# A float32 decoder layer on one core: some hidden tiles are split into halves ahead of DRAM, and the planner's numbers are set anew

## The chip, the cores and the metric

The kernel runs on one core of one Trainium2 chip. The metric is the device time of one execution in microseconds (us); lower is better. The engines are named PE (TensorE, the matmuls), PEld (its weight loads), DVE (VectorE), ACT (ScalarE), POOL (GpSimd) and SP (SyncE, which here issues most of the DMAs). DVE, ACT, POOL, SP and PE each run their own queue of instructions in order, and wait for each other by semaphores.

## The reference

One inference step of one decoder layer, for a prompt of 1024 tokens and 8 sample tokens that share the weights (1032 token columns, `T`; half of them with the samples is `TW` = 520, `HALF` is 512). `D_MODEL` is 1024, `D_FF` is 2816 (22 tiles of 128).

```python
def layer(x, pool_hist, conv_hist, start_pos, mk, mv, ...):
    h = rmsnorm(x, g_mix)
    u = h @ w_in
    a, val, gate = ...                       # 512 columns each
    glu = val * jax.nn.sigmoid(gate)
    ya = pool_mixer(a_ext, ...)              # window means 2/4/8/16, then a linear map for each group
    yb = conv_mixer(g_ext, ...)              # depthwise conv of width 31, LayerNorm, silu
    x = x + jnp.concatenate([ya, yb], axis=-1) @ w_out
    x = x + cross_attn(rmsnorm(x, g_attn), mk, mv, w_q, w_o)      # 4 heads, 256 memory tokens
    h = rmsnorm(x, g_ffn)
    x = x + (jax.nn.silu(h @ w_gate) * (h @ w_up)) @ w_down
    return x, ...
```

The memory's K and V are `rmsnorm(mem) @ w_k` and `@ w_v` for the prompt, and come from a cache for the samples. A last RMSNorm gives the outputs; all is float32.

## The kernel before, in words

**Precision.** Each matmul runs as three passes, high by high, high by low and low by high (`PASSES`). So each operand is held as two halves, in an operand tile (`op_r`, tag `op`, of which there are 19). Function `split` makes them: a copy to the high half (L400, on ACT or POOL) and a subtract to the low half (L411, on DVE or POOL). Function `split_by_dma` spares DVE: ACT writes the high half and its negative (L422), and a DMA on POOL's queue adds the source once more from DRAM onto the negative (L429), which leaves the low half.

**Order.** Nothing is issued in the order of the source. Each operation is recorded with its cost on each engine that could do it, and a planner lists them by priority, with the text `ORDER` as the order of the pieces, and with leads (`LEAD`), factors on the costs (`MARGINS`), `SLACK` and `BIAS` that say how far ahead a load or a split is put. The outcome is one fixed list for each engine; buffers of a tag (`op` 19, `raw` 3, `scr` 3, `acc` 1) go round among tiles as they come free.

**Stages.** First the projections and mixers (pieces A, m, g, v, s, C, D, M, W), with the memory's K (K0 to K3: matmuls `kps<-memg,w` L891, evacuated to `kf` by DVE L895) and V beside them, up to about 200 us of the span. There DVE also does the depthwise convolution: taps (L725), for the samples a short set (`side`, `cs`, `y`, L681 to L684), window sums (`win`, L855 to L869). Then output projection, attention (`pv`, evacuated to `oo` by L1131) up to about 537 us.

**Gated tiles** (pieces S, T, P and the rest up to about 931 us): 22 tiles of the hidden dimension, each by seven products over halves of the tokens and of the model (a Strassen-type scheme; functions `seven` and `others`). `to_hidden` stores the result: of the first 16 tiles, in pairs, seven blocks for each chunk of four tiles to DRAM `hb` (`to_blocks`; block numbers A11 = 4, S1 = 3, A12 = 0, S2 = 5, S3 = 6, S4 = 2, A22 = 1), of the last six (16 to 21) plain values to DRAM `hd`.

**Down stage** (o, u, x, y pieces, about 920 to 1070 us): 16 units, `down(u)`, chunk `u // 4`, four units for each. A unit loads a raw block of w_down (`dr`, tag `raw`), makes four sums and differences (`dt`, L1555, on POOL or DVE), and splits `dt` into `dV` and `dr` into `dW`. `down_blocks` loads the seven blocks of a chunk (`hs<-hb`, a scratch tile) and splits each into an operand tile `hb`. Which of them go through `split_by_dma` is in this line of it:

```python
            if b in DOWN_ORDER[: (0, 2, 4, 4)[c]]:
```

The products (`pr`, L1371) are evacuated into `x` and `pp` by DVE (L1387, added) or ACT (L1391, copied). **Last stage:** `hidden_load` loads the last six tiles (`ht<-hd`) and splits them by DMA into `ho`; `last_down` multiplies them (`fd` L1714), and the final norm writes `out_yT`.

Of the kernel before, what the change touches and what calls it, by code (L numbers as in the profile page):

```python
# [74 lines left out]
TW = HW[1]  # L75
A12, A22, S4, S1, A11, S2, S3 = range(7)
# [185 lines left out]
def hybrid_step_kernel(ctx: ExitStack, tc: tile.TileContext, io):  # L262
# [29 lines left out]
    def f32(ap):  # L292
        return ap.bitcast(F32)
# [81 lines left out]
    def dma(out, in_, nbytes, r=(), w=()):  # L375

        add({"SP": 0.05}, lambda e: e.dma_start(out(), in_()), r, w, nbytes=nbytes)
# [39 lines left out]
    def split_by_dma(dst, key, src, n, r, again, again_keys, pool_too=False):  # L417


        def scaled(e, p, src, factor):  # L420
            if e is nc.scalar:
                e.activation(dst(p), src, AF.Copy, scale=factor)  # L422
            else:
                e.tensor_scalar(dst(p), src, factor, 1.0, ALU.mult, ALU.mult)

        either = {"ACT": act(n), "Pool": pool_ts(n)} if pool_too else {"ACT": act(n)}
        add(either, lambda e: scaled(e, 0, src(), 1.0), r, [key(0)])
        add(either, lambda e: scaled(e, 1, f32(dst(0)), -1.0), [key(0)], [key(1)])
# [1001 lines left out]
    def kept(f, q):  # L1430

        return lambda: he[f][:, q]

    def times_value(f, q):
        if f in he:
            combine(kept(f, q), (he[f], q), part(f, q), (su[f], q), part(f, 2 + q), (su[f], 2 + q), ALU.mult, HW[q])
        else:
            times(f, q, part(f, 2 + q), (su[f], 2 + q))

    def to_blocks(f, first, count, src, keys):  # L1440
        c, j = f // 4, f % 4 // 2
# [136 lines left out]

# [51 lines left out]
    hops = []  # L1630

    def hidden_load(f):
        t = scr(f"ht{f}", (P, 2, TW))
        dma(lambda: t[:], lambda: hd[f - FIRST_LAST], 8 * P * TW, r=[("hd", f)], w=[(t,)])
        ho = op_r(f"ho{f}", (P, 2, 2, TW))
        split_by_dma(lambda p: ho[:, p], lambda p: (ho, p), lambda: t[:], 2 * TW, [(t,)], lambda: hd[f - FIRST_LAST], [("hd", f)])
        hops.append(ho)
# [258 lines left out]
```

## Time and profile before

| | us |
|---|---|
| median of three runs | 1162.25 |
| the runs | 1160.59, 1162.25, 1166.04 |
| the profiled execution | 1161.49 |
| its span | 1159.6 |
| PE busy | 1125.3 (97%) |
| DVE busy | 926.2 (80%) |
| ACT busy | 522.6 (45%) |
| POOL busy | 247.6 (21%) |
| mean granted clock of PE | 0.997 |

Busy is the time in which an engine has an instruction in work, over the whole span. A row of the timeline reads: start, length, engine, line, operation, output and inputs, shape, count; a bracket at its end says how long the engine stood idle just before it and what ended that. A row of the table by stage gives busy us and instruction count for each engine in a stretch.

### The profile page before, as it was taken

What the parts mean: (1) busy time and instruction counts of PE and PEld (TensorE: products, weight loads), DVE (VectorE), ACT (ScalarE), POOL (GpSimd) and SP (SyncE); (2) the same over time, 40 slices, a digit from 0 to 9 for tenths busy, and PEclk for the clock granted to TensorE, in tenths of its full rate; (3) what the DMA queues carried; (4) which work ended last, traced back from release to release, by engine and by line L of the source; (5) the groups of instructions that cost most, each with busy time, mean ns of one, the idle gap of its engine ahead of it and who ended that gap; (6) DMA issues with size and microseconds to landing.
All of it is one profiled execution on the core that took longest, in us unless ns stands there. A gap on an engine that the chain in (4) does not pass through costs nothing.

```text
span 1159.6 us, 19434 instructions
## 1 busy us (share of the span) xinstructions
PE 1125.3 (97%) x7736; PEld 1067.6 (92%) x7736; DVE 926.2 (80%) x1548; ACT 522.6 (45%) x718; POOL 247.6 (21%) x297
## 2 busy tenths in 40 slices
PE   9999989999999989999999999999999999999996
PEld 8899978999999979998999999999999999888996
DVE  7999999867359886879888887788867797879744
ACT  7666647455135552554232322233222455544633
POOL 3569853131101102122000000000000124332101
PEclk9999999999999999999999999999999999999999
DMA  7235595526386776422332233322323698678712
GB/s 303 75 81 126 114 253 172 194 81 204 134 282 201 230 250 247 124 79 74 119 120 83 106 132 112 119 83 102 129 76 131 229 296 237 169 195 218 172 56 92
DMA packets 60170, 179.69 MB, mean 155 GB/s; under 512 B 7792, under 2 KB 11568, under 8 KB 58800
## 3 DMA queue, kind: packets, MB, share of 16 engines
q1 hardware_dynamic: 53392, 157.56, 38.8%
q0 software_dynamic: 6256, 20.54, 10.2%
q8 instruction: 60, 0.98, 0.4%
q10 hardware_dynamic: 432, 0.36, 0.1%
q14 instruction: 30, 0.25, 0.1%
HBM read 144.66 MB, written 33.78 MB: 154 GB/s over the span
## 4 chain that ended last, share of the span: by engine, by line
PE 58%; DVE 12%; DMA 8%; issue 4%; ACT 2%; POOL 1%; SPq 0%; DVEq 0%; POOLq 0%; ACTq 0%
PE pr L1371 38%; PE po L512 5%; PE fd L1714 4%; PE ob L512 4%; PE oa L512 3%; DMA dr<-in_w_dn 3%; PE ps L512 2%; DMA xa<-x1d 1%; DVE x L1387 1%; DVE spcache_k L1165 1%; DMA hs<-hb 1%; DVE spcache_v L1165 1%; PE vps L969 1%; DVE hb L411 1%; DVE dV L411 1%
## 5 line engine op out<-in xcount | busy, mean ns | idle before, releaser
L1371 PEld LDWEIGHTS pr<-ab,wTb 128*128 128x128 f32 x1056 | 124.4, 190 | 2.2
L1371 PE MATMUL pr<-ab,wTa 128*128 128x260 f32 x1056 | 125.2, 275 | 0.9 <-DVE su L1387 0.9
L1371 PEld LDWEIGHTS pr<-ab,wTa 128*128 128x128 f32 x1056 | 123.1, 190 | 2.3 <-DVE su L1387 1.1
L1371 PE MATMUL pr<-ab,wTb 128*128 128x260 f32 x1056 | 124.8, 275 | 0.0
L1371 PE MATMUL pr<-ab,wG 128*128 128x512 f32 x528 | 121.2, 380 | 0.4 <-DVE wG L411 0.4
L512 PE MATMUL ps<-xop,w 128*128 128x344 f32 x720 | 106.0, 310 | 2.5 <-DVE w L411 1.5
L1371 PEld LDWEIGHTS pr<-ab,wG 128*128 128x128 f32 x528 | 96.6, 189 | 12.6 <-DVE wG L411 0.8
L512 PEld LDWEIGHTS ps<-xop,w 128*128 128x128 f32 x720 | 105.0, 189 | 3.0 <-DVE w L411 1.7
L1387 DVE TENSOR_TENSOR su<-pr,su 128x520 f32<-128x520 f32 (+1 forms) x112 | 77.4, 692 | 36.6 <-PE pr L1371 35.3
L1371 PEld LDWEIGHTS pr<-hb,dV 128*128 128x128 f32 x768 | 93.1, 190 | 4.4 <-DVE x L1387 1.9
L1371 PE MATMUL pr<-hb,dV 128*128 128x260 f32 x768 | 93.7, 275 | 1.5 <-DVE x L1387 1.5
L512 PE MATMUL ps<-xq,w 128*128 128x344 f32 x576 | 88.0, 311 | 1.0 <-DMA w<-in_w_q 1.0
L512 PEld LDWEIGHTS ps<-xq,w 128*128 128x128 f32 x576 | 84.2, 189 | 1.3 <-DMA w<-in_w_q 1.3
L512 PEld LDWEIGHTS po<-oo,w 128*128 128x128 f32 x576 | 84.0, 189 | 0.9 <-DVE oo L1131 0.6
L512 PE MATMUL po<-oo,w 128*128 128x344 f32 x576 | 84.5, 310 | 0.3 <-DVE oo L1131 0.2
L725 DVE SCALAR_TENSOR_TENSOR cacc<-glu,vec,cacc 128x511 f32<-128x511 f32 (+14 forms) x116 | 76.9, 740 | 0.0
L1371 PE MATMUL pr<-hb,dW 128*128 128x512 f32 x288 | 70.7, 382 | 4.9 <-DVE x L1387 3.8
L400 ACT ACTIVATE w<-raw 128x1024 fp32r<-128x1024 f32 (+1 forms) x37 | 35.0, 949 | 74.3 <-PE po L512 21.0
L1398 POOL MEMSET su<- 128x16 f32 x22 | 2.4, 111 | 294.0 <-PE pr L1371 248.8
L1714 PE MATMUL fd<-ho,w 128*128 128x260 f32 (+1 forms) x432 | 64.3, 311 | 0.0
L1714 PEld LDWEIGHTS fd<-ho,w 128*128 128x128 f32 x432 | 59.8, 190 | 4.4 <-issue 0.5
L1371 PEld LDWEIGHTS pr<-hb,dW 128*128 128x128 f32 x288 | 50.8, 189 | 11.0 <-DVE x L1387 4.1
(311 smaller groups left out, 2173.0 us busy)
## 6 DMA issues: line engine op xcount, KB each, us to landing
gr<-in_w_gu SPq DMA_DIRECT2D x44, 512.0 KB, 3.3
hb<-su SPq DMA_DIRECT2D x8, 1040.0 KB, 4.6
hs<-hb SPq DMA_DIRECT2D x16, 520.0 KB, 5.0
dr<-in_w_dn SPq DMA_DIRECT2D x16, 512.0 KB, 5.2
spcache_k<-in_cache_k SPq DMA_DIRECT2D x12, 512.0 KB, 5.8
hs<-hb SPq DMA_DIRECT2D x12, 512.0 KB, 5.9
raw<-in_w_in SPq DMA_DIRECT2D x10, 512.0 KB, 4.1
hb<-he SPq DMA_DIRECT2D x8, 520.0 KB, 2.8
```

What stands on the lines that cost most here:

```text
L400: e.activation(dst(0), src(), AF.Copy, scale=1.0 if gain is None else gain)
L411: e.tensor_tensor(dst(1), src(), f32(dst(0)), ALU.subtract)
L512: e.matmul(placed(ps[:, c, :CW]), w[:, wi, cols], turns(x[:, xi, c * CW : (c + 1) * CW]), start=first and p == 0, stop=last and p == 2)
L725: e.scalar_tensor_tensor(acc[h][:, n:], src[:, : HALF - n], w, acc[h][:, n:], ALU.mult, ALU.add)
L969: e.matmul(placed(ps[:, m]), memg[k // 4][:, xi, k % 4, m * P : (m + 1) * P], turns(w[:, wi, col : col + 512]), start=(k == 0 and p == 0), ...
L1165: e.scalar_tensor_tensor(piece[:, b], piece[:, b], 1.0, bc[:, b], ALU.mult, ALU.mult, accum_out=out(m)[:, first + b : first + b + 1])
L1371: e.matmul(placed(bank(c)), w[:, wi, cols(j)], turns(xs[0](j, xi)[:, c * n : (c + 1) * n]), start=onto is None and j == 0 and p == 0, stop ...
L1387: from_sums(sums, "DVE", dve, lambda e, src, sl: e.tensor_tensor(as_banks(o(sl), src), src, as_banks(a(sl), src), op), [akey], [okey])
L1398: add({"Pool": 0.12}, lambda e: e.memset(o(), 0.0), [], keys)
L1714: e.matmul(placed(view(i)), w[:, wi, col : col + P], turns(hops[k][:, xi, half, lo - half * HALF + i * width // count : lo - half * HALF + ...
```

## The change

The matmuls stay the same in kind and number. Three things change.

1. Of the last six gated tiles, five (17 to 21) are split before they are stored, and of the blocks for the down stage six: 2, 3 and 6 of chunk 1, 6 of chunk 2, 4 and 5 of chunk 3. A new function `split_here` does it: ACT copies the high half to a tile of tag `acc`, DVE subtracts it in place, and both halves are stored. They are loaded as they are into the operand tile, by two DMAs of SP, with no work of ACT, DVE or POOL behind. `hd` and `hb` in DRAM get a dimension for the half.
2. Which blocks are split by DMA add: the first 0, 1, 0 and 5 of `DOWN_ORDER` for chunks 0 to 3, instead of 0, 2, 4 and 4. As blocks 4 and 5 of chunk 3 are split ahead, the adds that are really issued are 0, 1, 0 and 3. (The entries 0 and 1 that `BY_DMA` gains for `w_in` change nothing: these two blocks go through another function.)
3. The planner's numbers: `ORDER`, `LEAD`, `BIAS`, `SLACK`, `MARGINS`. PE's two cost constants only get names.

By the order of the instructions, DVE has 13 more (nine subtracts of 1040 columns, four of 520; low halves of `hb` stay 18 in all, 7, 3, 6 and 2 for the chunks instead of 7, 5, 3 and 3); adds `hb<-hb` fall from 10 to 4, `ho<-hd` from 6 to 1; SP has 26 more DMAs.

```diff
-BY_DMA = {"w_in": (3, 4, 6, 7, 9, 10, 11), "w_k": (2, 3, 5), "w_o": (4, 5, 6), "w_out_a": (1,), "w_out_b": (3,), "w_q": (4, 5, 6), "w_v": (0, 7), "w_dn": (18, 19), "w_dn2": (1,)}
+BY_DMA = {"w_in": (0, 1, 3, 4, 6, 7, 9, 10, 11), "w_k": (2, 3, 5), "w_o": (4, 5, 6), "w_out_a": (1,), "w_out_b": (3,), "w_q": (4, 5, 6), "w_v": (0, 7), "w_dn": (18, 19), "w_dn2": (1,)}
-LEAD = {"w_k": 2, "w_v": 3, "w_out_a": 15, "w_q": 15, "w_in": 1, "w_out_b": 12, "w_o": 8}
+LEAD = {"w_k": 2, "w_v": 4, "w_out_a": 14, "w_q": 26, "w_in": 6, "w_out_b": 11, "w_o": 9}
-BIAS = {"evac": 0, "prep": 40, "load": 0}
+BIAS = {"evac": 0, "prep": 60, "load": 0}
+DOWN_BY_DMA = (0, 1, 0, 5)
+SPLIT_BLOCKS = ((), (2, 3, 6), (6,), (4, 5))
+SPLIT_FIRST = (17, 18, 19, 20, 21)
-SLACK = {"Pool": 0.3, "ACT": 0.15, "DVE": 0.05, "PE": 0.05}
+SLACK = {"Pool": 0.214, "ACT": 0.15, "DVE": 0.043, "PE": 0.051}
-    "down": {"DVE": (1.0, 0.083)},
+    "down": {"DVE": (0.97, 0.083)},
...
+    def split_here(name, n, src, keys):
+        hi = buf(name, "acc", (P, n, TW), F32R)
+        add({"ACT": act(n * TW)}, lambda e: e.activation(hi[:], src(), AF.Copy), keys, [(hi,)])
+        add({"DVE": dve(n * TW)}, lambda e: e.tensor_tensor(src(), src(), f32(hi[:]), ALU.subtract), keys + [(hi,)], keys, lock=True)
+        return hi
...
     def down_blocks(c, which):
+            if b in SPLIT_BLOCKS[c]:
+                o = db[c, b] = op_r(f"hb{c}_{b}", (P, 2, 2, n))
+                for p in range(2):
+                    dma(lambda o=o, p=p: f32(o[:, p]), lambda again=again, p=p: again(p=p), 8 * P * n,
+                        r=[("hb", c, b, j, p) for j in range(2)], w=[(o, p)])
+                continue
...
-            if b in DOWN_ORDER[: (0, 2, 4, 4)[c]]:
-                split_by_dma(part, key, src, 2 * n, [(t,)], again, [("hb", c, b, j) for j in range(2)])
+            if b in DOWN_ORDER[: DOWN_BY_DMA[c]]:
+                split_by_dma(part, key, src, 2 * n, [(t,)], again, kept_keys)
...
     def hidden_load(f):
+        if f in SPLIT_FIRST:
+            for p in range(2):
+                dma(lambda p=p: f32(ho[:, p]), lambda p=p: hd[f - FIRST_LAST, p], 8 * P * TW, r=[("hd", f, p)], w=[(ho, p)])
+            return
```

How the order moves shows at three places (names carry a chunk, unit or tile number and then the number of the tile's buffer; the lines of the changed kernel are four higher).

SP's queue in the down stage, before: from the raw weight of unit 6 (`dr6`) to that of unit 7 (`dr7`), with the loads `hs2_` of chunk 2 between them.

```order
L377 DMA dr6_9576<-in_w_dn 128x1024 [waits DMAHW0_49,DMAHW4_49,DVE_49,Pool_49]
L377 DMA hs2_4_9624<-hb_85 128x2x512 [waits DMAHW7_49,DVE_49,Activation_49]
L377 DMA hs2_3_9638<-hb_85 128x1040 [waits DMAHW2_49,DVE_49]
L377 DMA hs2_0_9657<-hb_85 128x2x512 [waits DMAHW3_49,DVE_49]
L377 DMA hs2_5_9670<-hb_85 128x1040 [waits DMAHW5_49,Activation_49]
L377 DMA hs2_6_9696<-hb_85 128x1040 [waits DMAHW6_49,DMAHW1_49,Activation_49]
L377 DMA dr7_9701<-in_w_dn 128x1024 [waits DVE_49]
```

The same place in the changed kernel, where `hb1_6` and `hb1_2` are operand tiles of chunk 1 that are loaded as halves:

```order
L381 DMA dr6_9611<-in_w_dn 128x1024 [waits DMAHW0_49,DVE_49,Pool_49]
L381 DMA hb1_6_9627<-hb_85 128x1040 [waits DMAHW5_49,PE_49]
L381 DMA hb1_6_9627<-hb_85 128x1040 [waits DMAHW6_49]
L381 DMA hb1_2_9639<-hb_85 128x2x512 [waits DMAHW7_49,PE_49]
L381 DMA hb1_2_9639<-hb_85 128x2x512
L381 DMA hs2_0_9679<-hb_85 128x2x512 [waits DMAHW1_49,DVE_49]
L381 DMA dr7_9705<-in_w_dn 128x1024 [waits DMAHW2_49,DVE_49]
```

Between the two raw weights there are five loads as before, but four of them are halves for chunk 1 and wait for PE, and most of chunk 2's loads have moved elsewhere. Ahead of `dr11` five loads become six, ahead of `dr15` three become five.

ACT's queue around the first evacuation of the down stage (`x2_0<-pr`), before:

```order
L400 ACTIVATE dW1_9211<-dr1_9007 128x256
L400 ACTIVATE hb0_2_9222<-hs0_2_9124 128x1024 [waits DMAHW1_49]
L400 ACTIVATE dV1_9226<-dt1_9180 128x1024 [waits DVE_49,Pool_49]
L400 ACTIVATE hb0_1_9236<-hs0_1_9155 128x1040 [waits DMAHW2_49]
L1391 ACTIVATE x2_0_9116<-pr2556_9228 128x512 [waits DMAHW0_49,PE_49]
L1423 ACTIVATE su21_8971<-su21_8971 128x520 [waits DVE_49,Activation_49]
```

And now:

```order
L404 ACTIVATE dW1_9256<-dr1_9051 128x256
L404 ACTIVATE hb0_2_9270<-hs0_2_9200 128x1024 [waits DMAHW7_49]
L1395 ACTIVATE x2_0_9161<-pr2597_9274 128x512 [waits PE_49]
L1427 ACTIVATE su21_8885<-su21_8885 128x520 [waits DVE_49,Activation_49]
L404 ACTIVATE dV1_9329<-dt1_9224 128x1024 [waits Pool_49]
L404 ACTIVATE hb0_1_9337<-hs0_1_9261 128x1040 [waits DMAHW5_49]
```

The evacuation now comes ahead of the copies for `dV1` and `hb0_1`.

DVE's queue around the low half of the third weight tile of K2's group (`w20`), before:

```order
L725 SCALAR_TENSOR_TENSOR cacc3_1_1482<-glu2_993,vec_68,cacc3_1_1482 128x499 [waits DVE_49]
L725 SCALAR_TENSOR_TENSOR cacc3_0_1477<-glu2_993,vec_68,cacc3_0_1477 128x498 [waits DVE_49]
L725 SCALAR_TENSOR_TENSOR cacc3_1_1482<-glu2_993,vec_68,cacc3_1_1482 128x498 [waits DVE_49]
L725 SCALAR_TENSOR_TENSOR cacc3_0_1477<-glu2_993,vec_68,cacc3_0_1477 128x497 [waits DVE_49]
L855 COPY win3_1648<-win3_1648 128x2x4 [waits Pool_49]
L856 TENSOR_TENSOR win3_1648<-win3_1648 128x2x508
L411 TENSOR_TENSOR w20_1673<-raw20_1590,w20_1673 128x1024 [waits DMAHW0_49,Activation_49]
L867 TENSOR_TENSOR win3_1648<-win3_1648,cnt_75 128x2x8 [waits DVE_49]
```

And now, the rows up to it (its own, `L415 ... w20`, is the next):

```order
L415 TENSOR_TENSOR kT0_1656<-kf1_1714,kT0_1656 128x512 [waits Activation_49]
L859 COPY win3_1679<-win3_1679 128x2x2 [waits Pool_49]
L860 TENSOR_TENSOR win3_1679<-win3_1679 128x2x510
L685 COPY side_216<-glu2_992 128x8
L686 TENSOR_TENSOR cs2_1747<-side_216,vec_68 128x248 [waits DVE_49]
L687 TENSOR_REDUCE y2_1122<-cs2_1747 128x8 [waits DVE_49]
L688 TENSOR_SCALAR y2_1122<-y2_1122,vec_68 128x8 [waits DVE_49]
L859 COPY win3_1679<-win3_1679 128x2x4
L860 TENSOR_TENSOR win3_1679<-win3_1679 128x2x508
L871 TENSOR_TENSOR win3_1679<-win3_1679,cnt_75 128x2x8 [waits DVE_49]
L872 TENSOR_REDUCE win3_1679<-side_216 128x8
L873 SCALAR_TENSOR_TENSOR win3_1679<-win3_1679,a1_531 128x1032 [waits DVE_49]
```

The low half of `kT`, one sample convolution and a window's mean (L871 to L873) are now ahead of the weight's low half, and in turn they no longer stand behind it.

More of the change, by code (lines that the diff above doesn't have):

```diff
@@ L41 @@
 ORDER = (
[5 rows of a table removed]
[5 rows of a table added]
 )
-BY_DMA = {"w_in": (3, 4, 6, 7, 9, 10, 11), "w_k": (2, 3, 5), "w_o": (4, 5, 6), "w_out_a": (1,), "w_out_b": (3,), "w_q": (4, 5, 6), "w_v": (0, 7), "w_dn": (18, 19), "w_dn2": (1,)}
+BY_DMA = {"w_in": (0, 1, 3, 4, 6, 7, 9, 10, 11), "w_k": (2, 3, 5), "w_o": (4, 5, 6), "w_out_a": (1,), "w_out_b": (3,), "w_q": (4, 5, 6), "w_v": (0, 7), "w_dn": (18, 19), "w_dn2": (1,)}
 WIDE = ("w_k", "w_v")
-LEAD = {"w_k": 2, "w_v": 3, "w_out_a": 15, "w_q": 15, "w_in": 1, "w_out_b": 12, "w_o": 8}
+LEAD = {"w_k": 2, "w_v": 4, "w_out_a": 14, "w_q": 26, "w_in": 6, "w_out_b": 11, "w_o": 9}
 LAST_SPANS = ((0, 512), (512, 260), (772, 260))
-BIAS = {"evac": 0, "prep": 40, "load": 0}
+BIAS = {"evac": 0, "prep": 60, "load": 0}
 ALL_SAMPLES = (1, 6, 7)
+DOWN_BY_DMA = (0, 1, 0, 5)
+SPLIT_BLOCKS = ((), (2, 3, 6), (6,), (4, 5))
+SPLIT_FIRST = (17, 18, 19, 20, 21)
+PE_FIXED, PE_COLUMN = 0.0135, 0.000417
 SCORES_MM = (12, 13, 14, 15)
-SLACK = {"Pool": 0.3, "ACT": 0.15, "DVE": 0.05, "PE": 0.05}
+SLACK = {"Pool": 0.214, "ACT": 0.15, "DVE": 0.043, "PE": 0.051}
 MARGINS = {
     "early": {"PE": (0.93, 0.0), "DVE": (0.93, 0.0), "Pool": (1.0, 0.0), "ACT": (1.0, 0.0)},
-    "gated": {"Pool": (1.02, 0.0), "DVE": (1.0, 0.04), "PE": (0.97, 0.0), "ACT": (1.1, 0.0)},
-    "down": {"DVE": (1.0, 0.083)},
-    "last": {"PE": (0.93, 0.0), "DVE": (1.0, 0.083)},
+    "gated": {"Pool": (0.99, 0), "DVE": (1.02, 0.04), "PE": (0.98, 0), "ACT": (1.08, 0)},
+    "down": {"DVE": (0.97, 0.083)},
+    "last": {"PE": (0.94, 0.08), "DVE": (1.03, 0.123)},
 }
@@ L317, in pe @@
     def pe(n, count=1):
-        return (0.0135 + 0.000417 * n) * count
+        return (PE_FIXED + PE_COLUMN * n) * count
     def pe32(n):
@@ L352, in hybrid_step_kernel @@
     x2d = dram.tile([KT, P, T], F32, name="x2d")
-    hd = dram.tile([FF_TILES - FIRST_LAST, P, 2, TW], F32, name="hd")
-    hb = dram.tile([CHUNKS, 7, P, 2, TW], F32, name="hb")
+    hd = dram.tile([FF_TILES - FIRST_LAST, 2, P, 2, TW], F32, name="hd")
+    hb = dram.tile([CHUNKS, 2, 7, P, 2, TW], F32, name="hb")
     qd = dram.tile([HEADS, NS, 256], F32, name="qd")
@@ L1438, in times_value @@
             times(f, q, part(f, 2 + q), (su[f], 2 + q))
+    def split_here(name, n, src, keys):
[3 more added lines that the diff above has]
+        return hi
     def to_blocks(f, first, count, src, keys):
         c, j = f // 4, f % 4 // 2
-        dma(lambda: hb[c, first : first + count, :, j].rearrange("b p t -> p b t"), src, 4 * P * TW * count, r=keys,
-            w=[("hb", c, b, j) for b in range(first, first + count)])
+        parts = [(first, count)] if not any(b in SPLIT_BLOCKS[c] for b in range(first, first + count)) else [
+            (b, min(2, first + count - b)) for b in range(first, first + count, 2)]
+        for b, n in parts:
+            at, pk = (lambda b=b, n=n: src()[:, b - first : b - first + n]), keys[b - first : b - first + n]
+            if b in SPLIT_BLOCKS[c]:
+                hi = split_here(f"bh{f}_{b}", n, at, pk)
+                dma(lambda b=b, n=n: hb[c, 0, b : b + n, :, j].rearrange("b p t -> p b t"), lambda hi=hi: f32(hi[:]), 4 * P * TW * n,
+                    r=[(hi,)], w=[("hb", c, x, j, 0) for x in range(b, b + n)])
+            dma(lambda b=b, n=n: hb[c, 1, b : b + n, :, j].rearrange("b p t -> p b t"), at, 4 * P * TW * n, r=pk,
+                w=[("hb", c, x, j, 1) for x in range(b, b + n)])
     def start(f, q, single=ms_buf):
@@ L1485, in to_hidden @@
             combine(kept(e, 1), (he[e], 1), kept(e, 0), (he[e], 0), part(f, 3), (k, 3), ALU.subtract)
+            combine(part(f, 2), (k, 2), part(f, 0), (k, 0), kept(e, 1), (he[e], 1), n=HALF)
             to_blocks(f, A11, 2, lambda: he[e][:], [(he[e], 0), (he[e], 1)])
-            combine(part(f, 2), (k, 2), part(f, 0), (k, 0), kept(e, 1), (he[e], 1), n=HALF)
             to_blocks(f, A12, 4, lambda: su[f][:], [(k, q) for q in range(4)])
@@ L1492, in to_hidden @@
         else:
-            dma(lambda: hd[f - FIRST_LAST], lambda: su[f][:, 0:2], 8 * P * TW, r=[(k, 0), (k, 1)], w=[("hd", f)])
+            whole = [(k, 0), (k, 1)]
+            if f in SPLIT_FIRST:
+                hi = split_here(f"hh{f}", 2, lambda: su[f][:, 0:2], whole)
+                dma(lambda: hd[f - FIRST_LAST, 0], lambda: f32(hi[:]), 8 * P * TW, r=[(hi,)], w=[("hd", f, 0)])
+            dma(lambda: hd[f - FIRST_LAST, 1], lambda: su[f][:, 0:2], 8 * P * TW, r=whole, w=[("hd", f, 1)])
     def seven(f):
@@ L1568, in down_blocks @@
             n = WIDTH[b]
+            again, kept_keys = (lambda b=b, n=n, p=1: hb[c, p, b][:, :, :n]), [("hb", c, b, j, 1) for j in range(2)]
+            if b in SPLIT_BLOCKS[c]:
+                o = db[c, b] = op_r(f"hb{c}_{b}", (P, 2, 2, n))
[3 more added lines that the diff above has]
+                continue
             t = scr(f"hs{c}_{b}", (P, 2, n))
-            again = lambda b=b, n=n: hb[c, b][:, :, :n]
-            dma(lambda t=t: t[:], again, 8 * P * n, r=[("hb", c, b, j) for j in range(2)], w=[(t,)])
+            dma(lambda t=t: t[:], again, 8 * P * n, r=kept_keys, w=[(t,)])
             o = db[c, b] = op_r(f"hb{c}_{b}", (P, 2, 2, n))
             part, key, src = (lambda p, o=o: o[:, p]), (lambda p, o=o: (o, p)), (lambda t=t: t[:])
-            if b in DOWN_ORDER[: (0, 2, 4, 4)[c]]:
-                split_by_dma(part, key, src, 2 * n, [(t,)], again, [("hb", c, b, j) for j in range(2)])
+            if b in DOWN_ORDER[: DOWN_BY_DMA[c]]:
+                split_by_dma(part, key, src, 2 * n, [(t,)], again, kept_keys)
             else:
@@ L1632, in hidden_load @@
     def hidden_load(f):
+        ho = op_r(f"ho{f}", (P, 2, 2, TW))
+        hops.append(ho)
+        if f in SPLIT_FIRST:
+            for p in range(2):
+                dma(lambda p=p: f32(ho[:, p]), lambda p=p: hd[f - FIRST_LAST, p], 8 * P * TW, r=[("hd", f, p)], w=[(ho, p)])
+            return
         t = scr(f"ht{f}", (P, 2, TW))
[L1634 to L1637, printed above, removed]
+        dma(lambda: t[:], lambda: hd[f - FIRST_LAST, 1], 8 * P * TW, r=[("hd", f, 1)], w=[(t,)])
+        split_by_dma(lambda p: ho[:, p], lambda p: (ho, p), lambda: t[:], 2 * TW, [(t,)], lambda: hd[f - FIRST_LAST, 1], [("hd", f, 1)])
     parts = {
```

10 rows, old and new, of the table ORDER are left out of this document.

## The prediction

> **What bounds the kernel now.** I read the page first (who is busy), then the table by stage (where TensorE, PE, stands idle), then PE's own waits in those stages, and last the queue behind each wait. All durations are from the profiled execution: 1161.49 us with a span of 1159.6, which is 0.76 under the median of the three runs, 1162.25.
>
> The page's first part, and the table by stage (start and end; then busy us and instruction count of PE, its weight loads, DVE, ACT, POOL; PE's granted clock; DMA share; GB/s):
>
> ```profile
> PE 1125.3 (97%) x7736; PEld 1067.6 (92%) x7736; DVE 926.2 (80%) x1548; ACT 522.6 (45%) x718; POOL 247.6 (21%) x297
> ...
> 90.00:200.00 110.00, 104.59 (x674) 97.77 (x674) 108.09 (x163) 66.60 (x83) 72.15 (x55) 0.98 0.62 163
> 537.00:931.00 394.00, 393.86 (x2826) 373.63 (x2826) 321.20 (x449) 120.08 (x156) 7.55 (x36) 1.00 0.34 119
> 931.00:1068.00 137.00, 130.82 (x923) 122.96 (x924) 118.09 (x172) 72.66 (x91) 47.17 (x54) 1.00 0.78 216
> ```
>
> PE bounds the kernel: 34 us of the span (1159.6 - 1125.3) are not PE, and the matmuls are the same after the change. So every gain is one of PE's idle stretches. Three stages matter. 90 to 200 us: DVE is busy 108.09 of 110, so DVE's queue sets the end there and PE's waits are its echo. 537 to 931, the gated tiles: PE lacks 0.14 us in all. 931 to 1068, most of the down stage: PE lacks 6.2. PE's waits there, in brackets with what ended them:
>
> ```profile
> 931.95 1.56 PE L1371 MATMUL pr<-hb,dW 128*128 128x512 f32 x6 [1.09 <-ACT x L1391]
> 985.26 1.53 PE L1371 MATMUL pr<-hb,dW 128*128 128x512 f32 x6 [0.21 <-DVE x L1387]
> 989.74 1.56 PE L1371 MATMUL pr<-hb,dW 128*128 128x512 f32 x6 [1.60 <-DVE x L1387]
> 1024.58 1.61 PE L1371 MATMUL pr<-hb,dV 128*128 128x260 f32 x12 [1.47 <-DVE x L1387]
> 1029.13 1.56 PE L1371 MATMUL pr<-hb,dW 128*128 128x512 f32 x6 [0.32 <-DVE x L1387]
> 1058.87 1.56 PE L1371 MATMUL pr<-hb,dW 128*128 128x512 f32 x6 [1.64 <-DVE x L1387]
> ```
>
> They sum to 6.33. Five of the six name DVE's evacuation of PSUM (L1387), but DVE itself waited. Rows of the queues of POOL and DVE, then SP's, then the chain of waits (start, length, kind):
>
> ```profile
> 1021.41 0.73 POOL L1555 TENSOR_TENSOR dt<-dr 128x256 f32<-128x256 f32 x1 [8.12 <-DMA dr<-in_w_dn]
> 983.58 0.93 DVE L1555 TENSOR_TENSOR dt<-dr,dt 128x256 f32<-128x256 f32 x1 [3.06 <-POOL dt L1555]
> 1056.04 0.43 DVE L1555 TENSOR_TENSOR dt<-dr 128x256 f32<-128x256 f32 x1 [2.06 <-DMA dr<-in_w_dn]
> ...
> 963.31 7.75 SPq L377 DMA_DIRECT2D hs<-hb  x5
> 971.11 6.18 SPq L377 DMA_DIRECT2D dr<-in_w_dn  x2
> 1001.77 7.95 SPq L377 DMA_DIRECT2D hs<-hb  x5
> 1009.80 6.28 SPq L377 DMA_DIRECT2D dr<-in_w_dn  x2
> 1041.16 4.45 SPq L377 DMA_DIRECT2D ht<-hd  x3
> ...
> 971.11 10.74 DMA dr<-in_w_dn
> 1009.80 11.45 DMA dr<-in_w_dn
> 1048.87 7.05 DMA dr<-in_w_dn
> ```
>
> So one story is told three times: a chunk's loads `hs` go out in a burst, the raw weight `dr7` (then `dr11`, `dr15`) is issued behind them, lands 10.74, 11.45 and 7.05 us later, the sum `dt` waits for it in the queue of POOL or DVE, and the evacuations that PE needs stand behind that sum. The two slow landings have software adds `hb<-hb` beside them, in the third stretch only one `ho<-hd` is.
>
> **The change, part by part.**
>
> *Splits in the gated stage* (13 times a high copy on ACT and a low subtract on DVE: nine of 1040 columns, four of 520). DVE's subtract of 1040 took 1.23 and a 512-wide form 0.68 (rows below), so 9 x 1.23 + 4 x 0.68 = 13.8 us of DVE, and 9 x 1.05 + 4 x 0.57, about 12, of ACT (a copy of 1024 or 1040 columns and one of 512, below). Both have the room: in 394 us DVE is idle 72.8 and ACT 274. What hides it is PE's own work of 393.86; if DVE were late at a tile's end, each 1.23 would show. The last split (tile 21) falls after 931, where DVE is all but full; chunk 1 has two lows fewer on DVE there (3 for 5, -2.5). Cost 0; bounds 0 and +2.5 (two 1040 subtracts on a full DVE).
>
> ```profile
> 962.02 1.23 DVE L411 TENSOR_TENSOR hb<-hs,hb 128x1040 fp32r<-128x1040 f32 x1
> 970.58 0.68 DVE L1387 TENSOR_TENSOR x<-pr,x 128x512 f32<-128x512 f32 x1
> 930.37 1.05 ACT L400 ACTIVATE hb<-hs 128x1040 fp32r<-128x1040 f32 x1
> 931.33 0.57 ACT L1391 ACTIVATE x<-pr 128x512 f32<-128x512 f32 x1
> 930.00:960.00 30.00, 28.91 (x208) 27.27 (x207) 28.99 (x44) 18.14 (x26) 8.73 (x10) 1.00 0.90 275
> ```
>
> *The evacuation on ACT at 931.* PE waited 1.09 for `x`, which stood behind a `dV` copy and an `hb` copy (1.05). In the new order it comes ahead of both. -1.09; bounds -1.09 and 0 (if the next evacuation, on DVE, is as late).
>
> *Adds that go.* Adds of `hb` fall from 10 to 4 and of `ho` from 6 to 1: 11 x 0.52 = 5.7 MB leave the software queue, and as much is loaded by SP instead. From 900 to 1160 us:
>
> ```profile
> q1 hardware_dynamic: 14321, 37.48, 41.1%
> q0 software_dynamic: 3376, 10.05, 22.5%
> ```
>
> A software MB takes 22.5/10.05 = 2.24% of the engines in these 260 us, a hardware MB 1.10%; 5.7 x 1.14 = 6.5%, about 17 us of engine time, comes free. None of it is on PE's path except through `dr`:
>
> First stall (`dr7`). Still five loads lie between `dr6` and `dr7`, but no add is left in chunk 2 to share the engines; and two of DVE's lows, for which the old burst waited, are gone. A landing like the third one (7.05 for 10.74) is 3.7 us earlier, more than the 3.06 that DVE waited. -1.81; bounds -1.81 and 0.
>
> Second (`dr11`). Six loads for five lie ahead, and three of the four adds of chunk 3 stay; DVE gets 6 lows for 3 in chunk 2. Half: -0.9; bounds -1.79 and +1.5 (one more load, 7.95/5 = 1.6).
>
> Third (`dr15`). One `ht` and four `ho` lie ahead for three `ht`: 0; bounds -1.64 and +3.0 (two loads of 4.45/3).
>
> *The new wait.* `hs` went into a scratch tile freed by ACT or DVE. A direct `hb` or `ho` goes into an operand tile that PE must have released, so SP's queue stands until then, and behind it stand the next `hs` and `dr`. No row of before shows this; nearest is a `dr` stall (1.6 on PE), in up to five places. I take +0.5, as the order leaves several groups of PE between load and use; bounds 0 and +8.
>
> *The early stage.* The first 34 us are the same. Behind that, DVE's rows (start, length):
>
> ```profile
> 83.78 0.76 DVE L723 TENSOR_SCALAR cacc<-glu,vec 128x512 f32<-128x512 f32 x1 [0.97 <-ACT y L733]
> 165.72 0.16 DVE L867 TENSOR_TENSOR win<-win,cnt 128x16 f32<-128x16 f32 x1
> 166.11 1.23 DVE L869 SCALAR_TENSOR_TENSOR win<-win,a 128x1032 f32<-128x1032 f32 x1
> 168.52 0.17 DVE L681 COPY side<-glu 128x8 f32<-128x8 f32 x1
> 169.63 0.23 DVE L684 TENSOR_SCALAR y<-y,vec 128x8 f32<-128x8 f32 x1
> ...
> 163.76 0.38 PE L891 MATMUL kps<-memg,w 128*128 128x256 f32 x2
> 165.85 5.67 PE L891 MATMUL kps<-memg,w 128*128 128x256 f32 x46 [1.71 <-DVE w L411]
> 175.63 3.61 PE L912 MATMUL pmap<-win,wmap 128*128 128x344 f32 x6 [2.09 <-DVE kf L895]
> 175.00:177.50 2.50, 1.87 (x4) 1.16 (x5) 1.80 (x2) 1.86 (x3) 2.03 (x2) 0.67 0.28 105
> 177.50:180.00 2.50, 2.50 (x8) 1.71 (x7) 2.47 (x7) 1.66 (x2) 0.00 (x0) 0.64 0.00 0
> ```
>
> Ahead of the low half of K2's weight DVE now has a window mean (165.72 to 167.34, 1.6), a sample convolution (168.52 to 169.86, 1.3) and one `kT` low (0.7, as another 512-wide row), less one tap (0.7): +2.9. So PE waits 1.71 + 2.9 = 4.6 in K2. Behind it, DVE has about 1.9 less up to `kf`, for which PE waits next (two sample convolutions fewer, a window's steps more): there the lag is 1.0. Ahead of all that DVE loses a 0.97 wait and has 1.3 more rows: +0.3. Together +1.3 at 175.63, the last PE wait of this stage, so nothing behind it absorbs the lag. Of it I take +1.0, since the 2.09 before it gets shorter and with it, perhaps, the dip of the clock: 2.5 x 0.33 + 2.5 x 0.36 = 1.7 us. Bounds -1.7 (no lag, no dip) and +4.3 (the lag, and K2's 46 matmuls at 0.65 as well: 5.67/0.65 - 5.67 = 3.0).
>
> [...]
>
> *Attention* (325 to 433) is permuted. Its largest waits:
>
> ```profile
> 420.31 5.42 PE L1126 MATMUL pv<-pT,vv 128*128 128x512 f32 x24 [1.50 <-DVE oo L1131]
> 427.25 3.04 PE L1126 MATMUL pv<-pT,vv 128*128 128x512 f32 x13 [1.02 <-DVE oo L1131]
> ```
>
> The cache products still stand just ahead of the `oo` evacuations. -0.5 (a fifth of 2.52); bounds -2.5 and +2. The last stage: its `ho` come without ACT or POOL, but PE waits there 0.41 and 0.59 for other things: 0.
>
> **Sum:** -1.09 - 1.81 - 0.9 + 0 + 0.5 + 1.0 - 0.5 = -2.8. 1161.49 - 2.8 = 1158.7.
>
> **Rivals.**
>
> *More is won.* With 17 us of engine time free, all `dr` land in time: -6.33 for the down stage, no lag in the early one, -2.5 in attention: 1152.7. For it: POOL's 8.12 and DVE's 3.06 waits hang on transfers alone. Against it: five or six loads still lie ahead of each `dr`.
>
> *No net change.* The burst, not the adds, makes `dr` late; only the 1.09 goes, and the early lag eats it: 1161.49 - 1.09 + 1.0 = 1161.4. For it: the third stall came with three loads and hardly an add.
>
> *Slower: SP's queue stands for PE.* If an operand tile is released less than one landing (5 to 7 us) before the first use of its block, the load is late for PE and holds `dr` too. The three stalls stay and the five new places cost 1.64 each: 1161.49 - 1.09 + 8.2 + 1.0 = 1169.6. For it: the old burst at 963.31 shows that SP's queue does stand. Against it: 19 operand tiles for 7 blocks of a chunk. It decides from two such places on, whose 3.3 undo the forecast.
>
> *The clock falls in K2*: the early stage costs 4.3 instead of 1.0: 1162.0. For it: a longer wait than any that PE had there; against it: none after 1.71.
>
> **How the numbers follow.** Forecast 0.39 (its own range 1156 to 1161), more won 0.27, no net change 0.14, the clock in K2 0.08, SP's queue 0.12. A change of 0.5%, 5.8 us, is about what a measurement of this kernel can tell from none: under 1156.4 is faster, above 1168.1 slower. Faster: the 0.27 and a fifth of the forecast's chance, 0.35. Slower: five sixths of SP's queue, 0.10, since with four places it stands at 1168.0. Same: the rest, 0.55. The range, 1150.5 to 1167.5, leaves out a third of the second case at its lower end and SP's queue at its upper, 2 in 10 together.
>
> **What would show it.** Right: no PE wait of 1 us at about 932 and none at `dr7`; POOL's wait at `dr11` under 8.12; in K2 one PE wait of 3.5 to 5 us for `w` L415; gated tiles without PE waits. Wrong: waits of PE on DMA `hb` or `ho`, SP waiting for PE `pr` for over 3 us (the queue); granted clock at 0.65 for longer than 5 us near 170 (K2); waits after 1000 us all gone (more won).

## The result, and the profile after

The changed kernel takes 1166.8 us (median of six runs) against 1160.78 before (six runs too): ratio 1.005, interval 1.0026 to 1.0075. I had forecast 1158.7. The profiled execution took 1166.73, its span is 1165.0 (before 1159.6).

The page's first part and three rows of the table by stage, of the changed kernel:

```profile
PE 1129.3 (97%) x7736; PEld 1072.3 (92%) x7736; DVE 949.3 (81%) x1560; ACT 511.5 (44%) x706; POOL 243.5 (21%) x290
...
90.00:200.00 110.00, 95.47 (x592) 90.30 (x592) 107.80 (x154) 55.65 (x69) 63.29 (x52) 0.92 0.56 143
537.00:931.00 394.00, 393.93 (x2821) 373.16 (x2822) 332.98 (x466) 135.13 (x174) 9.22 (x35) 1.00 0.35 123
931.00:1068.00 137.00, 135.71 (x968) 128.13 (x967) 124.76 (x181) 59.46 (x79) 44.53 (x50) 1.00 0.75 248
```

PE won 4.9 us in the down stage (135.71 busy, it had 130.82) and lost 9.1 between 90 and 200 us (95.47 for 104.59), where its granted clock also fell to 0.92. The same matmuls begin 11 to 12 us later from there to the gated tiles, and the span ends 5.4 later: the rest of the kernel gave 6 back. PE's waits, first the early ones and the start of the gated tiles, then the two that are left above half a us in the down stage:

```profile
141.94 5.62 PE L895 MATMUL kps<-memg,w 128*128 128x256 f32 x48 [0.89 <-DVE a L881]
157.66 8.37 PE L895 MATMUL kps<-memg,w 128*128 128x256 f32 x48 [10.10 <-DVE a L881]
179.13 7.03 PE L895 MATMUL kps<-memg,w 128*128 128x256 f32 x46 [2.52 <-DVE w L415]
532.37 2.43 PE L1375 MATMUL pr<-ab,wG 128*128 128x512 f32 x10 [0.30 <-DVE wG L415]
...
945.59 1.61 PE L1375 MATMUL pr<-hb,dV 128*128 128x260 f32 x12 [0.57 <-DVE pp L1391]
1017.84 1.56 PE L1375 MATMUL pr<-hb,dW 128*128 128x512 f32 x6 [0.66 <-DVE x L1391]
```

In the kernel before, the rows of K1, of `a` and of the start of the gated tiles were:

```profile
147.96 5.60 PE L891 MATMUL kps<-memg,w 128*128 128x256 f32 x48 [1.56 <-DVE a L877]
146.59 1.22 DVE L877 TENSOR_TENSOR a<-ps,Rx 128x1032 f32<-128x1032 f32 x1
520.90 2.42 PE L1371 MATMUL pr<-ab,wG 128*128 128x512 f32 x10 [0.39 <-DVE wG L411]
```

The big wait is in K1, ahead of K2: 10.10 us (it was 1.56) for DVE's evacuation of `a`. DVE was not idle; it was busy 107.80 of 110. So the question is what it was busy with. Rows of its queue from a little earlier on:

```profile
81.01 1.99 DVE L688 TENSOR_SCALAR y<-y,vec 128x8 f32<-128x8 f32 x1
115.02 4.86 DVE L851 COPY side<-a 128x8 f32<-128x8 f32 x1
145.15 2.66 DVE L685 COPY side<-glu 128x8 f32<-128x8 f32 x1
148.30 0.41 DVE L687 TENSOR_REDUCE y<-cs 128x8 f32<-128x248 f32 x1
148.75 1.75 DVE L688 TENSOR_SCALAR y<-y,vec 128x8 f32<-128x8 f32 x1
156.29 1.22 DVE L881 TENSOR_TENSOR a<-ps,Rx 128x1032 f32<-128x1032 f32 x1
172.60 2.48 DVE L688 TENSOR_SCALAR y<-y,vec 128x8 f32<-128x8 f32 x1
```

All but `a` and the TENSOR_REDUCE are instructions on eight columns that took microseconds; in the kernel before, the same lines took 0.16 to 0.52. Now look at POOL at the same times:

```profile
80.59 2.38 POOL L761 TENSOR_TENSOR t<-t,Rx 128x1032 f32<-128x1032 f32 x1 [0.57 <-ACT t L760]
115.10 1.39 POOL L712 TENSOR_TENSOR y<-y,cp 128x506 f32<-128x506 f32 x1
116.14 2.67 POOL L415 TENSOR_TENSOR w<-raw,w 128x1024 fp32r<-128x1024 f32 x1
118.46 6.36 POOL L712 TENSOR_TENSOR y<-y,cp 128x505 f32<-128x505 f32 x5
145.07 2.70 POOL L415 TENSOR_TENSOR w<-raw,w 128x1024 fp32r<-128x1024 f32 x1
148.01 2.46 POOL L415 TENSOR_TENSOR w<-raw,w 128x1024 fp32r<-128x1024 f32 x1 [0.24 <-ACT w L404]
172.52 2.52 POOL L415 TENSOR_TENSOR w<-raw,w 128x1024 fp32r<-128x1024 f32 x1
```

The long rows of DVE end where a POOL instruction ends: 81.01 + 1.99 = 83.00 against 82.97; 145.15 + 2.66 = 147.81 against 147.77; 148.75 + 1.75 = 150.50 against 150.47; 172.60 + 2.48 = 175.08 against 175.04; the 4.86 ends at 119.88, when the first of the five from 118.46 (6.36/5 = 1.27 each) ends at 119.73. So they look like standing and not work, although the profile counts it as busy; the experiments below test it. Ahead of `a` the four rows 1.99, 4.86, 2.66 and 1.75 are about 10 us longer than their usual 0.16 to 0.23, and the evacuation came 9.7 later than before (156.29 for 146.59).

### The profile page after: what moved, and what is told of

Read it like the earlier page. It is cut to its first block, busy times and chain, and to the rows that moved or that the text cites. A ratio compares the mean times of both kernels' runs of the same rounds, so it can differ in the third digit from the quotient of the medians.

```text
span 1165.0 us, 19498 instructions
## 1 busy us (share of the span) xinstructions
PE 1129.3 (97%) x7736; PEld 1072.3 (92%) x7736; DVE 949.3 (81%) x1560; ACT 511.5 (44%) x706; POOL 243.5 (21%) x290
## 4 chain that ended last, share of the span: by engine, by line
PE 69%; DVE 21%; DMA 5%; issue 3%; ACT 2%; POOL 1%; DVEq 0%; SPq 0%; POOLq 0%; ACTq 0%
PE pr L1375 44%; PE po L516 7%; DVE cacc L729 6%; PE fd L1746 4%; PE oa L516 4%; PE ob L516 4%; DVE spcache_k L1169 2%; DMA spcache_k<-in_cache_k 1%; PE ps L516 1%; DVE xss L447 1%; PE kps L895 1%; DVE spcache_v L1169 1%; PE vps L973 1%; PE sc L1072 1%; DMA hs<-hb 1%
## 5 line engine op out<-in xcount | busy, mean ns | idle before, releaser
L729 DVE SCALAR_TENSOR_TENSOR cacc<-glu,vec,cacc 128x501 f32<-128x501 f32 (+14 forms) x116 | 77.0, 736 | 0.1
L404 ACT ACTIVATE wG<-gr 128x1024 fp32r<-128x1024 f32 x22 | 23.3, 1057 | 94.4 <-PE pr L1375 82.3
L1427 ACT ACTIVATE su<-su 128x512 f32<-128x512 f32 (+1 forms) x44 | 27.6, 629 | 75.8 <-DVE su L1399 75.7
```

What stands on the lines that cost most here:

```text
L404: e.activation(dst(0), src(), AF.Copy, scale=1.0 if gain is None else gain)
L729: e.scalar_tensor_tensor(acc[h][:, n:], src[:, : HALF - n], w, acc[h][:, n:], ALU.mult, ALU.add)
L1427: add({"ACT": act(HW[q])}, lambda e: e.activation(o(), o(), AF.Silu), [k], [k], func=AF.Silu)
```

## The experiments

**The same order, another form for the small instructions.** If only the form of these rows changes and the order of all engines stays, the order's rows are told from the standing. First I wrote them with two SBUF inputs:

```diff
-            e.tensor_copy(st_conv()[:, cg, :, 30], gb[:, i, SEQ:T])
+            e.tensor_tensor(st_conv()[:, cg, :, 30], gb[:, i, SEQ:T], gb[:, i, SEQ:T], ALU.max)
...
-            e.tensor_scalar(yb[:, i, SEQ:T], yb[:, i, SEQ:T], vcol(V_CB, cg), None, ALU.add)
+            e.tensor_tensor(yb[:, i, SEQ:T], yb[:, i, SEQ:T], vcol(V_CB, cg).to_broadcast([P, NS]), ALU.add)
...
-        add({"DVE": 0.07}, lambda e: e.tensor_copy(st_pool()[:, g, :, 15], ab[:, ai, SEQ:T]), [ak, (side, "pool")], [(side, "pool", g)])
+        add({"DVE": 0.07}, lambda e: e.tensor_tensor(st_pool()[:, g, :, 15], ab[:, ai, SEQ:T], ab[:, ai, SEQ:T], ALU.max), [ak, (side, "pool")], [(side, "pool", g)])
```

> The changed kernel with the same order word for word; only the three small SBUF-to-SBUF forms of DVE that took 4.86, 2.66, 1.75 and 2.48 us in the early stage (two 128x8 copies to `side`, one 128x8 tensor_scalar on `y`) are written as tensor_tensor with two inputs (max of a value with itself; addition of a broadcast column), which gives the same values. Theory port (a one-input SBUF copy of DVE stands until the POOL instruction beside it ends): these rows fall under 0.5 us each, DVE gets back about 10 us ahead of the evacuation of `a` and of K2's weight, PE's wait of 10.10 at 157.66 falls under 3, and the time falls by 9 to 11 us, to 1156 to 1158. Theory order (the rows that the new order puts ahead of the evacuation make it late, and the long copies only wait for something else): the replaced rows stay as long, the 10.10 stays, 1165 to 1168.

It took 1168.12, ratio to before 1.0055 (1.0040 to 1.0069): nothing gained. DVE's rows, then PE's wait:

```profile
114.77 4.86 DVE L851 TENSOR_TENSOR side<-a 128x8 f32<-128x8 f32 x1
144.91 2.64 DVE L685 TENSOR_TENSOR side<-glu 128x8 f32<-128x8 f32 x1
148.48 1.75 DVE L688 TENSOR_TENSOR y<-y,vec 128x8 f32<-128x8 f32 x1
...
157.40 7.02 PE L895 MATMUL kps<-memg,w 128*128 128x256 f32 x48 [10.08 <-DVE a L881]
```

The rows kept their length to 0.02 us under another operation. So my first idea of the mechanism (it is the copy that stands) was wrong, but the rows still end with POOL's. The same edit in the kernel before is the control:

> The same replacement in the kernel before, whose copies were not long (0.16 to 0.52 us). Theory port: within 1 us of before, since little stood there. If the replacement were worth something by itself (a cheaper form), it would be 3 us or more faster here too. Theory order: no change.

Ratio 0.9999 (0.9986 to 1.0012), as both theories had it.

**A form with one SBUF input.** In the changed kernel a `tensor_reduce` of DVE took its 0.41 beside a POOL subtract (148.30 above). So I wrote both copies as a reduce over an axis of one, and the bias addition as a reduce of pairs (of the edit, the new lines of the sample set):

```diff
+            e.tensor_reduce(st_conv()[:, cg, :, 30], gb[:, i, SEQ:T].unsqueeze(2), axis=AX.X, op=ALU.add)
...
+            e.tensor_reduce(tmp[:, at + NS : at + 2 * NS], vcol(V_CB, cg).unsqueeze(1).to_broadcast([P, NS, 1]), axis=AX.X, op=ALU.add)
+            e.tensor_reduce(yb[:, i, SEQ:T], tmp[:, at : at + 2 * NS].rearrange("p (two b) -> p b two", two=2), axis=AX.X, op=ALU.add)
```

> The changed kernel, same order; the small sample forms of DVE on SBUF are now written as tensor_reduce over an axis of one or two elements (one SBUF input each): the two copies to `side` as one reduce each, the bias addition on `y` as a reduce of the bias and one of the pair. In the first run of experiments the same rows with two SBUF inputs stayed as long as before (4.86, 2.64, 1.75, 2.49), to within 0.1 us of the end of the POOL instruction beside them, while a tensor_reduce of DVE ran in 0.41 at 148.03 beside a POOL subtract. Theory shared read side (a DVE instruction that reads SBUF twice, or copies SBUF to SBUF, stands until POOL's instruction ends; one with one SBUF input does not): the rows fall to 0.2 to 0.4 each, PE's wait of 10.1 in K1 to under 3, the time by 9 to 11 us to 1156 to 1158. Theory any small DVE instruction waits for POOL: the rows stay, 1166 to 1168. Theory order: the rows fall, but the evacuation is as late and the 10 us stay: 1165 to 1168.

It took 1159.39, ratio to before 0.9982 (0.9965 to 0.9999); the changed kernel stood at 1.005. DVE's rows, POOL's beside them, and PE's waits:

```profile
111.98 0.16 DVE L853 TENSOR_REDUCE side<-a 128x8 f32<-128x8 f32 x1
137.40 0.16 DVE L685 TENSOR_REDUCE side<-glu 128x8 f32<-128x8 f32 x1
137.60 2.87 DVE L686 TENSOR_TENSOR cs<-side,vec 128x248 f32<-128x248 f32 x1
140.83 0.15 DVE L689 TENSOR_REDUCE cs<-vec 128x8 f32<-128x8 f32 x1
141.01 0.17 DVE L690 TENSOR_REDUCE y<-cs 128x8 f32<-128x16 f32 x1
146.98 1.22 DVE L883 TENSOR_TENSOR a<-ps,Rx 128x1032 f32<-128x1032 f32 x1
165.26 3.25 DVE L875 SCALAR_TENSOR_TENSOR win<-win,a 128x1032 f32<-128x1032 f32 x1
...
137.48 5.22 POOL L415 TENSOR_TENSOR w<-raw,w 128x1024 fp32r<-128x1024 f32 x2
165.07 2.35 POOL L415 TENSOR_TENSOR w<-raw,w 128x1024 fp32r<-128x1024 f32 x1 [0.49 <-ACT w L404]
...
148.35 7.10 PE L897 MATMUL kps<-memg,w 128*128 128x256 f32 x48 [4.72 <-DVE a L883]
169.70 8.10 PE L897 MATMUL kps<-memg,w 128*128 128x256 f32 x46 [3.67 <-DVE w L415]
```

The reduces take 0.15 to 0.17. The two for the bias ran inside POOL's second subtract (from about 140.1 to 142.7), and the one for `a` stood to POOL as the copy of 4.86 did, with POOL's next instruction 0.08 behind its start. Of the 9 to 11 us that I expected 7.4 came. One reason is that the next instruction that reads SBUF twice now met POOL. `cs` (usually 0.42) took 2.87: it stood for the first of POOL's two subtracts (137.48 to about 140.1) and then ran its 0.42. The window's mean (usually 1.23) took 3.25: POOL's subtract ended at 167.42, and the mean 1.1 later. In these rows neither the size (8 to 1032 columns) nor the operation alone decides. Those that stood read SBUF twice (`cs` 2.87, the mean 3.25, the copy of `a` as `tensor_tensor` 4.86), or took one SBUF operand to SBUF as a copy (4.86, 2.66) or a `tensor_scalar` (1.75). The reduces did not stand (0.15 to 0.41), and neither did the convolution taps (0.66 each throughout), which keep one operand in PSUM.

The evacuation of `a` is at 146.98 here, and was at 146.59 in the kernel before: 0.4 later, with the 2.45 us that `cs` stood still ahead of it. So the new order's own rows added nothing to `a`; its 9.7 us were standing. The rows of one piece of work in its three forms say the same: 1.75 as `tensor_scalar`, 1.75 as `tensor_tensor`, and 0.15 and 0.17 as two reduces for the bias addition, each beside a POOL subtract; 4.86, 4.86 and 0.16 for the copy of `a`. What DVE and POOL share in these rows no run shows; the runs show which forms stood.

The early stage as a whole is not back to where it was: the gated tiles of this run begin 5.2 later than before (526.14 for 520.90). PE reaches K1 2.8 earlier than before and waits 4.72 there for 1.56, and then 3.67 in K2; its granted clock falls to 0.85 from 150 to 155 us and to 0.50 from 170 to 175, and K1 and K2 together take 3.9 longer.

One row of the three, alone:

> The changed kernel, same order, with only the copy of `a` to `side` (the row of 4.86 us) as a tensor_reduce; the other two forms stay. Theory shared read side: that row falls to 0.2 and DVE comes 4.7 earlier to the rest, PE's 10.1 wait to about 5.5, the time 4 to 5 us below the changed kernel, 1161.5 to 1163.5, unless the next DVE rows now meet other POOL instructions. Theory order: no change, 1166 to 1168.

```profile
115.32 0.16 DVE L851 TENSOR_REDUCE side<-a 128x8 f32<-128x8 f32 x1
140.74 2.83 DVE L685 COPY side<-glu 128x8 f32<-128x8 f32 x1
144.50 1.78 DVE L688 TENSOR_SCALAR y<-y,vec 128x8 f32<-128x8 f32 x1
...
153.45 8.16 PE L895 MATMUL kps<-memg,w 128*128 128x256 f32 x48 [7.48 <-DVE a L881]
```

1163.3, ratio 1.0005 (0.9991 to 1.0019): 4.5 thousandths, about 5 us, for a row that was 4.7 too long. The others still meet POOL. PE's wait falls by 2.6 only, since PE too comes earlier to it.

The replacement in the kernel before shows that the form is worth little where nothing collides:

> The same replacement in the kernel before, whose rows of these lines sum to 3.0 us, of which 0.7 is above their usual 0.17. Theory shared read side: 0 to 1 us faster than before, 1159.5 to 1161. If the new form gains by itself, 3 us or more. Other theories: no change.

1159.14, ratio 0.9990 (0.9971 to 1.0008).

**The splits, and the numbers.** Which of them made the gain in the down stage?

```diff
-DOWN_BY_DMA = (0, 1, 0, 5)
-SPLIT_BLOCKS = ((), (2, 3, 6), (6,), (4, 5))
-SPLIT_FIRST = (17, 18, 19, 20, 21)
+DOWN_BY_DMA = (0, 2, 4, 4)
+SPLIT_BLOCKS = ((), (), (), ())
+SPLIT_FIRST = ()
```

> The changed planner numbers without splitting ahead: no tile or block is split ahead of DRAM, and the blocks by DMA add are 0, 2, 4, 4 again. The order up to the gated stage is that of the changed kernel. Theory splits (the 5 us gained in the down stage come from splitting ahead): the early 10 us wait stays, and the stalls of 1 to 2 us of PE between 931 and 1068 come back: 1169 to 1173. Theory numbers (they come from the new priorities and factors): 1165 to 1168, down stage without stalls over 1 us.

1174.9, ratio 1.0107 (1.0083 to 1.0131), above the range that I expected. The other half, splits with the old order text, leads, bias, slack and factors:

> The splits ahead and their DMA adds with the planner numbers of before (order text, leads, factors). The order up to the gated stage is that of the kernel before. Theory splits: early stage as before, PE idle in the down stage 1 to 2 us instead of 6.3: 1155 to 1157. Theory numbers: the stalls stay, 1159 to 1162. Either theory of the early stage expects no wait over 3 us of PE there.

1160.45, ratio 0.9987 (0.9974 to 0.9999): a gain, but of 0.1%, and not the 0.4% that I expected. To see both without the early standing, the reduce form went into both.

> The changed planner numbers without splitting ahead, and the replacement. That kernel took 1174.9 with the early wait of 10 us in it. Theory shared read side: 9 to 11 us less, 1164 to 1166, and what is left above before (about 4 us) is the down stage of the new numbers without splits. Theory order: 1173 to 1176.

1166.47, ratio 1.0038 (1.0016 to 1.0059), again a little above.

> The splits ahead with the planner numbers of before, and the replacement. Theory shared read side: as the run without the replacement (1160.45, ratio 0.9987), 0 to 1 us less: 1159 to 1160.5. Other theories: the same as without.

1158.66, ratio 0.9979 (0.9960 to 0.9998). So with the new numbers splitting ahead is worth 7.1 us (1166.47 to 1159.39), with the old ones 0.5 (1159.14 to 1158.66). The new numbers without the splits are worse than the old ones by 7.3. The traces say where: cut each at the start of the gated tiles (the row at 520.90 before).

| | gated tiles begin | from there to the end |
|---|---|---|
| before | 520.90 | 638.7 |
| splits alone (with the reduces; without) | 521.77; 522.51 | 637.3; 636.4 |
| new numbers alone (with; without) | 527.25; 536.61 | 637.8; 637.6 |
| both (with; without: the changed kernel) | 526.14; 532.37 | 633.0; 632.6 |

So most of the 7.3 is the early stage (6.3 in the trace); behind it the new numbers alone gain about 1 us and the splits alone 1.4 to 2.3, and both together about 6. Neither half makes the gain by itself; the two belong together. (One trace each, and the start of the gated tiles moved by 4 us between two runs of one early order, 532.37 and 536.61.)

**Old order early, new one late.** The last experiment takes the planner's numbers of before up to the gated tiles and the changed ones, with the splits, from there on. `ORDER`, `LEAD` and `BY_DMA` go back as a whole, since they reach no further: in the code `ORDER`'s pieces S, T and P are the attention's scores, transposes and products, and o, u, x and y its output projection, the squares of the result and its splits for the gated tiles; the gated tiles and the down stage are not in it. In the trace each engine's rows come in the order of before up to the first gated tiles (about 535 us or later) and, from 627 us at the latest, in that of the changed kernel. Of the edit:

```diff
...
+LATE_SLACK = {"Pool": 0.214, "ACT": 0.15, "DVE": 0.043, "PE": 0.051}
-                pick, slack = None, SLACK.get(e, 0.02)
+                pick, slack = None, (SLACK if free["PE"] < 500 else LATE_SLACK).get(e, 0.02)
...
     pg.margin, state["alone"] = MARGINS["gated"], True
+    BIAS["prep"] = 60
```

> The changed kernel with the order text, leads, bias and slack of before up to the gated tiles, and its own bias, slack and factors from there on, with the splits ahead. The order of every engine is word for word that of before up to the gated tiles, and that of the changed kernel from there on. Theory two parts (the early stage loses 11 us at the mark of 521 us, the rest gains 6): 1154 to 1156, faster than both. Theory coupled (the late order only fits behind the early one): 1159 to 1161.

1157.36 against 1162.46 of before on that chip: ratio 0.9958 (0.9941 to 0.9974). It is faster than both, though a little above the range that I expected. The profile (span 1153.9), three of PE's waits and one row by stage:

```profile
147.50 5.60 PE L896 MATMUL kps<-memg,w 128*128 128x256 f32 x48 [1.52 <-DVE a L882]
520.89 2.43 PE L1376 MATMUL pr<-ab,wG 128*128 128x512 f32 x10 [0.38 <-DVE wG L416]
1006.39 1.56 PE L1376 MATMUL pr<-hb,dW 128*128 128x512 f32 x6 [0.66 <-DVE x L1392]
...
931.00:1068.00 137.00, 135.93 (x968) 128.40 (x968) 126.35 (x186) 57.22 (x75) 41.74 (x45) 1.00 0.71 230
```

The gated stage begins at 520.89, where it did before (520.90), and the end is 5.7 earlier (5.1 by the medians): that is what the change is worth behind the early stage. With the reduce form on top:

> The kernel of the line above with the small sample forms as tensor_reduce. In the kernel before the replacement gave 0.1% at most (ratio 0.999): 1153 to 1156.

1156.21, ratio 0.9949 (0.9929 to 0.9968), not told apart from the one without it.

## Why the prediction was wrong

The direction was wrong: faster by 3 us was forecast, and it is slower by 6. That 1166.8 lies inside the stated range (1150.5 to 1167.5) is luck, for no term and no rival had this cause. Measured against the sum (-2.8 on 1161.49), two terms carry the difference.

*The early stage: +1.0 forecast, about +11 measured* (198.35 to 209.29 at the first `oa` product). This is the step that failed, in the part that reads "Ahead of all that DVE loses a 0.97 wait and has 1.3 more rows: +0.3": the evacuation of `a`, which lies there, came 9.7 late. I counted DVE's rows, each at the duration that it had before, and did not look at K1's wait for `a` at all. The count was not too small: without most of the standing `a` is 0.4 late. The durations were wrong. I looked at the order of DVE alone, and never laid POOL's beside it. In the kernel before, two of the sample sets (168.52 to 169.86, and one at 171.20) ran while POOL had nothing to do; this row of its queue was there to be read, and with it the first of two copies of `a` that showed the price in small (0.52 and 0.51 in place of 0.16):

```profile
175.10 0.19 POOL L855 COPY win<-win 128x2 f32<-128x2 f32 x1 [10.35 <-issue]
125.78 0.52 DVE L847 COPY side<-a 128x8 f32<-128x8 f32 x1
```

The new order put the sets and the copy of `a` beside POOL's additions and subtracts. The planner can keep a task of DVE apart from POOL's (tasks with `lock`), but the copy of `a` is entered without it at 0.07, so no plan keeps it apart from POOL. The sample sets have it, and met POOL all the same: at 145.15 DVE arrived 0.08 behind POOL's subtract of 145.07. I take that for a planned start that was off by a little, which no run shows. Whether a `lock` on the copy would have avoided the 4.86 was not tried.

The wait in K2 came as 2.52 (4.6 forecast), with the clock under it. My rival on the clock had the right kind of loss, but most of it came in another place, behind K1's 10.10; by stages of 2.5 us:

```profile
150.00:152.50 2.50, 0.00 (x0) 0.00 (x0) 2.50 (x5) 1.06 (x1) 0.74 (x2) 0.50 1.07 238
160.00:162.50 2.50, 2.50 (x14) 2.50 (x14) 2.50 (x5) 0.00 (x0) 0.32 (x1) 0.50 1.06 273
162.50:165.00 2.50, 2.50 (x20) 2.50 (x20) 2.50 (x5) 1.06 (x1) 2.42 (x4) 0.80 0.98 388
180.00:182.50 2.50, 2.50 (x16) 2.50 (x15) 2.43 (x7) 0.00 (x0) 0.00 (x0) 0.61 0.87 236
```

K1's 48 matmuls took 8.37 for 5.60 and K2's 46 took 7.03 for 5.67: 2.8 and 1.4 us. In the wait of 10.10 the clock was at 0.50 (150 to 152.5), and at 160 to 162.5 it still was; behind the 2.52 it fell to 0.61. In the kernel before it was at 0.67 and 0.64 from 175 to 180, about a wait of 2.09, and at 1.00 from 165 to 175, about one of 1.71. What length of wait is needed the runs do not show.

*Behind the early stage: -3.8 forecast with attention, about -5.5 measured.* Attention, permuted, cost 1.0 more (its output projection begins 11.9 late) where -0.5 was forecast; the rest gave about 6 for 3.3. Here the mechanism was right, and too small. The 1.09 at 932 is gone. So are the stalls at `dr7` (forecast so), at `dr11` (I had kept half) and at `dr15` (I had kept all of it); two waits of 0.57 and 0.66 are left of 6.33. The adds that went freed less than I had worked out. From 900 us to the end:

```profile
q1 hardware_dynamic: 17191, 46.82, 49.9%
q0 software_dynamic: 1408, 4.22, 9.3%
...
SPq L381 <- PE pr L1375: 7.8, 8, 3.8
```

A software MB still takes 9.3/4.22 = 2.20% in 265 us, a hardware MB 1.07%. But the hardware queue moved 9.3 MB more (46.82 for 37.48) and not 5.7, so 59.2% of 265 us stand against 63.6% of 260: about 9 us of engine time came free, not 17. The last row is SP's queue from 930 to 1065: it did stand for PE, 7.8 us in eight times, 3.8 at most, which is over the 3 that I had named as a sign of the slower rival; but no PE wait over half a us hung on a `dr`. That rival's time, 1169.6, came near the measured one with its mechanism absent.

*Hidden, as forecast:* the splits in the gated stage. DVE went from 321.20 to 332.98 busy and PE stayed at 393.93 of 394.

## What to carry to other kernels

A row that is moved need not keep its duration: lay the queue of the engine and that of the one for which it stood (here DVE for POOL, 4.86 us for a copy that took 0.16 to 0.52 before) side by side at the new place, and look for instructions of eight columns that take microseconds. Busy time in a profile may be standing; where the same line has rows of 0.17 and of 4.86, compare their ends with the neighbour's. And when a change is a bundle, a version that takes one stage from each side, as the last but one here, tests the account and was here also the better kernel.

## What was not expected of the hardware

DVE's copy at 115.02 did not get in at the end of the POOL instruction that it met: it let three pass (to 119.73, 4.86 us), while in the kernel before the copy at 125.78, which met POOL's pair from 124.72 (2.70), took 0.52. With the reduces, a `tensor_reduce` over an axis of one was a copy that did not stand, 0.15 us at 140.83 inside a POOL subtract.
